# Prompt attention: the value products of two neighbouring units in one run of TensorE and one PSUM bank

## The chip, the cores and the metric

The kernel runs on one core of one Trainium2 chip. The metric is device time in microseconds (us) of one execution. The core has five engines that each work through their own row of instructions in order, and wait for one another through semaphores: TensorE (PE, matmuls, with the weight loads shown apart as PEld), VectorE (DVE), ScalarE (ACT), GpSimd (POOL) and SyncE (SP, which issues DMAs).

## What is computed

The reference is one inference step of a decoder layer with two kinds of heads (forgetting attention and a matrix memory), for one prompt of 2048 tokens and for 64 new tokens of eight older sequences; then an output projection, layer norms and an MLP. The change touches only the forgetting attention of the prompt: 8 heads of 64 columns, 2048 queries and keys, causal, with a decay that is a difference of running sums of log forget values.

```python
def _fox_prompt(q, k, v, logf):
    L = jnp.cumsum(logf, axis=1).transpose(0, 2, 1)
    ...
    def block(args):
        q_i, L_i, i = args
        s = jnp.einsum('bqhd,bkhd->bhqk', q_i, k).astype(jnp.float32) * scale
        s = s + L_i[..., :, None] - L[:, :, None, :]
        q_pos = i * Q_BLOCK + jnp.arange(Q_BLOCK)
        s = jnp.where(k_pos[None, :] <= q_pos[:, None], s, -jnp.inf)
        p = jax.nn.softmax(s, axis=-1)
        return jnp.einsum('bhqk,bkhd->bqhd', p.astype(v.dtype), v)
    ...
...
    mix = jnp.concatenate([fox_h, mn.astype(x.dtype)], axis=-1) @ w_o
```

## The kernel before

The program has stages one after the other: projections and the matrix memory, then the prompt attention (`phase_b`), the output projection, the MLP. Beside them runs, in slices, the attention over the paged cache of the older sequences. A tile framework gives every tile its buffer from a ring of so many buffers (`bufs=`), adds the waits, and sets the order of each engine's row when the program is built, by a simulated timeline; on the chip each engine keeps to its row.

The prompt attention goes over 64 units: 8 heads (h) by 8 groups (g) of 256 queries. A unit (h, g) has the keys 0 to 256(g + 1) - 1, so its work grows with g. The loop over n issues `scores` of unit n, then `values` of unit n - 1 (LA = 1).

`scores`: for each of the unit's two rows of 128 queries and each 512 keys, two matmuls (L1028 and L1029) put the products of the split queries `qh`, `ql` with the rounded keys `ks` into a score bank `pS`; there are three such banks. DVE adds the decay `nl` (L1036; on the diagonal `nd`, with the causal mask, L1040), keeps the largest value of each row in `mx`, and writes the tile `S` in SBUF (7 buffers of 128 x 1024).

`values`: ACT takes the exponential of `S` in place, with the row sums as a by-product (L1057); DVE gathers them (L1058, `ls`). PE turns each 128 x 128 piece of `S` by a transpose (L1073) into `pt`, up to four pieces in a bank, three such banks. ACT (L1076) or DVE (L1078) copies them to `PT` (4 buffers of 128 x 4 x 256). When the unit's last transpose is issued, the value products follow (L1083): 2g + 2 matmuls with 64 columns of values `vn` against 256 queries, even key blocks in rows 0 to 63 of the bank `po`, odd ones in rows 64 to 127. Each of these fp32 matmuls leaves two records in the trace. There is one `po` bank. ACT copies its first half to `ot` (L1091) and DVE adds the second half (L1093). After every fourth unit `finish` scales by the reciprocal row sums, through a small round trip in DRAM (`drl`, `rl`), and stores the result (`dmix`).

Around these stand, in each head, the loads of the next head's keys, `kn`, in four pieces, and of each unit's queries `qn`, on SP's queue, with their splits: ACT rounds (L153, to `ks`, `qh`), DVE forms the remainder (L156, the lower half of `ks`, and `ql`). A key piece can be split once the buffer of keys is free. GpSimd forms `nd` and sums output weights of the MLP in DRAM.

The output projection reads its weights `w_o` through `raw()`, a ring named `wr` of five tiles of 128 x 1024; `half_wo` loads one of them. Before the change five such loads are in the program at n = 60, and SP's row has them among the first loads of the stage.

Places of the names: `raw` is

```python
        return pcw.tile([128, 1024], F32, name="wr", bufs=5)
```

and `tc.issue_after(turned.ins)` keeps a product behind the named transpose in PE's row.

Of the kernel before, what the change touches and what calls it, by code (L numbers as in the profile page):

```python
# [10 lines left out]
F32 = mybir.dt.float32  # L11
# [3 lines left out]
OP = mybir.AluOpType  # L15
# [37 lines left out]
def body(ctx, tc, I, O, stages):  # L53
    nc = tc.nc
    V, A, G, T, SY = nc.vector, nc.scalar, nc.gpsimd, nc.tensor, nc.sync
# [51 lines left out]
    last = {}  # L107
# [821 lines left out]
    for bi in range(4):  # L929
        g = block_a(bi)  # L930
# [20 lines left out]
    def phase_b():  # L951
        es = ExitStack()
        pb = es.enter_context(tc.tile_pool(name="pb", bufs=1, reuse_waits="tile"))
        ppb = es.enter_context(tc.tile_pool(name="ppb", bufs=1, space=PSUM, reuse_waits="tile"))
# [92 lines left out]
        def values(z, g, sc):  # L1047

            if z["h"] == 0 and g == 0:
                pad(pb, 64)  # L1050
            for i, (st, mx) in enumerate(sc):
                qt = 2 * g + i
                n = (qt + 1) * 128
                lp = pb.tile([128, 2], F32, name="lp", bufs=6)
                for k, sp in enumerate(st):
                    w = min(1024, n - k * 1024)
                    last["ACT"] = A.activation(sp[:, :w], sp[:, :w], AF.Exp, bias=mx[:, 7:8], accum_out=lp[:, k:k + 1])  # L1057
                V.tensor_reduce(z["ls"][:, qt:qt + 1], lp[:, :len(st)], axis=AX.X, op=OP.add)  # L1058

            po = ppb.tile([128, 256], F32, name="po", bufs=1)  # L1060
            nk = 2 * g + 2
            PTs = []
            for k0 in range(0, nk, 4):
                PT = pb.tile([128, 4, 256], F32, name="PT", bufs=4)
                PTs.append(PT)
                for i in range(2):
                    kk = min(4, 2 * g + i + 1 - k0)
                    if kk <= 0:
                        continue
                    pt = ppb.tile([128, 4, 128], F32, name="pt", bufs=3)  # L1070
                    for k in range(kk):
                        c = k0 % 8 * 128 + k * 128
                        turned = T.transpose(pt[:, k], sc[i][0][k0 // 8][:, c:c + 128], ident)  # L1073
                    dst = PT[:, :kk, i * 128:i * 128 + 128]
                    if i == 0 or (k0 // 4) % 2 != 0:
                        A.copy(dst, pt[:, :kk])  # L1076
                    else:
                        V.tensor_copy(dst, pt[:, :kk])  # L1078
            for k in range(nk):
                q0 = 128 if k == nk - 1 else 0  # L1080
                c = (k % 2) * 64
                with tc.issue_after(turned.ins):
                    last["PE"] = T.matmul(po[c:c + 64, q0:], z["vn"][:, k], PTs[k // 4][:, k % 4, q0:],  # L1083
                                          start=(k < 2), stop=(k >= nk - 2), skip_group_check=True)
            if g % 4 == 0:
                z["ot"] = pb.tile([64, 1024], F32, name="ot", bufs=2)
            od = z["ot"][:, (g % 4) * 256:(g % 4) * 256 + 256]
            if (z["h"], g) == units[-1]:
                V.tensor_copy(od, po[0:64])
            else:  # L1090
                A.copy(od, po[0:64])  # L1091
            q0 = 128 if g == 0 else 0
            V.tensor_tensor(od[:, q0:], od[:, q0:], po[64:128, q0:], op=OP.add)  # L1093
            if g % 4 == 3:
                finish(z, g // 4)

        def finish(z, half):

            h, ls, ot = z["h"], z["ls"], z["ot"]
            lr = pb.tile([128, 32], F32, name="lr", bufs=2)  # L1100
            V.reciprocal(lr, ls)
            lt = pb.tile([128, 32], F32, name="lt", bufs=2)
            V.transpose(lt, lr)
            o = half * 1024
            for a in range(4):
                SY.dma_start(drl[h, o:o + 1024].rearrange("(t a q) -> a t q", a=4, q=32)[a], lt[a * 32 + half * 8:a * 32 + half * 8 + 8])
            for q in range(2):
                rl = pb.tile([64, 512], F32, name="rl", bufs=2)
                SY.dma_start(rl, dap(drl, h * S + o + q * 512, [[0, 64], [1, 512]]))
                s = slice(q * 512, (q + 1) * 512)  # L1110
                end = (h, half) == (7, 1)
                (V if end else G).tensor_tensor(ot[:, s], ot[:, s], rl, op=OP.mult)
                (G if end else SY).dma_start(dmix[h // 2, (h % 2) * 64:(h % 2) * 64 + 64, o + q * 512:o + q * 512 + 512], ot[:, s])
# [15 lines left out]
        G.affine_select(dmask, dmask, pattern=[[-1, 128]], compare_op=OP.is_ge, fill=NEG, base=0, channel_multiplier=1)  # L1129
        keys(Z[0], 0, bf["kn"])  # L1130
        sc = {}
        w2_due = [0.0]
        LA = 1
        for n in range(len(units) + LA):
            if 10 <= n < 16 and acc[1] is not None:
                attend()
            w2_due[0] += 64 * (n % 8 // 2 + 1) / 130 if n >= 8 else 0
            while n and len(w2_done) < min(60 if False else 64, w2_due[0]):
                w2_sum()
            if n == 60:  # L1140
                wo.extend(half_wo(*q) for q in ((0, 0), (0, 1), (0, 2), (0, 3), (1, 0)))
            if n < len(units):
                h, g = units[n]
                sc[n] = scores(Z[h], g)
                if h == 0 and g % 2 == 0 and g < 6:
                    keys(Z[0], g // 2 + 1)
                if h < 7:
                    if g == 3:
                        Z[h + 1] = head(h + 1)
                        forget_values(Z[h + 1], 0, S)  # L1150
                    if g >= 4:
                        keys(Z[h + 1], g - 4)
                if n + 1 < len(units):
                    queries(Z[units[n + 1][0]], units[n + 1][1])
            if n >= LA:
                h, g = units[n - LA]
                values(Z[h], g, sc.pop(n - LA))
# [15 lines left out]
    def raw():  # L1173

        return pcw.tile([128, 1024], F32, name="wr", bufs=5)
# [9 lines left out]
    def w2_sum():  # L1185

        k = len(w2_done)
        w2_done.append(k)
        j, src, q, more = W2_SUMS[k // 8]
        with tc.issue_after(last["POOL"].ins):  # L1190
            G.dma_start(dw2[k % 8, j], src[k % 8, q], **({"accum_op": OP.add} if more else {}))

    def half_wo(hf, q):

        r = raw().rearrange("p (k c) -> p k c", k=2)
        SY.dma_start(r, I["w_o2"][hf, q].rearrange("p (k c) -> p k c", k=2))
        return r
# [445 lines left out]
def sample_attention(tc, I, O, ps_, pps, cst, ident, dnl, dR, dmix, dqb, vx, kx, pa):  # L1643
# [218 lines left out]
    def weights(b, u, hg):  # L1862

        z = state[b]
        if hg == 0:
            z["PT"] = ps_.tile([128, 2, 4, 4, 4, 8], F32, name="PTs", tag="PTs", bufs=1)
        PT = z["PT"]
        p = pps.tile([128, 4, 128], F32, name="sT", tag="sX", bufs=1)
        for f in range(4):
            T.transpose(p[:, f], z["U"][u][:, hg, f].rearrange("p k t -> p (k t)"), ident)  # L1870
        for f in range(4):
            (A.copy if f % 2 else V.tensor_copy)(PT[:, hg, f].rearrange("p g h q -> p h g q"),
                                                 p[:, f].rearrange("p (h g q) -> p h g q", g=4, q=8))
# [22 lines left out]
    def pv_step(b, kt, after):  # L1896
# [164 lines left out]
```

## Time and profile before

| what | value |
|---|---|
| runs, median of 3 | 3192.88 us (3190.92 to 3194.03) |
| profiled execution, span from first to last instruction | 3196.6 us (the record gives no other time for it) |
| mean granted clock of TensorE | 0.989 |
| DVE, ACT busy over the span | 65%, 45% |
| prompt attention in the trace | 869 to 1308 us |
| in that stretch, busy: PE, DVE, ACT | 418.0, 345.7, 330.5 of 439.0 us |
| its transposes (PE, L1073) | 1088 |
| its value products (PE, L1083), records | 1152 |

A row of the timeline gives the start, the duration, the engine, the line, the operation with output and inputs, and how many instructions it joins; in brackets stands the idle time before it and what ended that. The durations of matmuls overlap, so that the distance between two starts is the better price of one. A row of the windows gives the window, its length, and the busy time of PE, PEld, DVE, ACT and POOL with the number of instructions, then the granted clock (1.00 is full speed), the share of the DMA engines, and GB/s. A row of the waits gives the waiting instruction, the one that it waited for, the us in total, how often, and the longest.

### The profile page before, as it was taken

To read this page: it belongs to the slowest core of one execution; us is meant where nothing else is said; L and a number is where in the kernel's file an instruction comes from. 1 tells how busy PE (TensorE), PEld (TensorE's weight loads), DVE (VectorE), ACT (ScalarE), POOL (GpSimd) and SP (SyncE) were. 2 spreads that over 40 slices of the span, in tenths; PEclk is the share of its full clock that TensorE was granted. 3 is DMA by queue.
4 is the path that set the end of the run, shared out by engine and by line. 5 is a ranking of instruction groups with operands and counts; after the bars stand their busy time and mean duration, and the time that the engine had idled before them with its cause. 6 is when DMAs were issued, how large, how long until landed. Compare 5 with 4: busy or idle time off the path is not lost.

```text
span 3196.6 us, 53750 instructions
## 1 busy us (share of the span) xinstructions
PE 3103.8 (97%) x19869; PEld 2442.8 (76%) x19869; DVE 2081.3 (65%) x5025; ACT 1439.5 (45%) x2629; POOL 907.0 (28%) x976
## 2 busy tenths in 40 slices
PE   8999999999999999999999999999999999899998
PEld 8997787787667667777777777777766777698886
DVE  6956467465488778534657568565675665766667
ACT  3343244344387777422444445343444444344442
POOL 0121132423433333466333324333334111000000
PEclk9999999999999999999999999999999999999999
DMA  5565666877787865687877879878779766643231
GB/s 191 155 213 181 236 225 202 277 261 237 245 260 178 204 152 139 223 297 259 314 291 271 308 243 335 312 270 323 290 262 332 276 213 208 209 155 132 101 123 63
DMA packets 323615, 732.58 MB, mean 229 GB/s; under 512 B 63097, under 2 KB 153721, under 8 KB 322457
## 3 DMA queue, kind: packets, MB, share of 16 engines
q1 hardware_dynamic: 235928, 413.36, 39.3%
q0 software_dynamic: 83808, 304.91, 27.6%
q10 hardware_dynamic: 3616, 10.88, 0.9%
q8 instruction: 157, 2.57, 0.3%
q14 instruction: 106, 0.86, 0.1%
HBM read 676.20 MB, written 86.38 MB: 239 GB/s over the span
## 4 chain that ended last, share of the span: by engine, by line
PE 47%; DMA 4%; DVE 1%; issue 1%; POOL 1%; ACT 0%; DVEq 0%; POOLq 0%; ACTq 0%
PE ph L162 7%; PE ph L164 7%; PE ph L163 7%; PE py L162 6%; PE py L163 6%; PE py L164 6%; PE sO L1913 3%; DMA vt<-cache_v,idxV 2%; PE sQ L1801 2%; PE ph L169 1%; PE sT L1870 1%; DMA kT<-cache_k,idxK 1%; DMA xr<-cache_v,idxV 0%; DVE wl L156 0%; PE pw L163 0%
## 5 line engine op out<-in xcount | busy, mean ns | idle before, releaser
L156 DVE TENSOR_TENSOR wl<-wr,wh 128x1024 fp32r<-128x1024 f32 x300 | 366.3, 1223 | 241.3 <-ACT wh L153 240.3
L153 ACT ACTIVATE wh<-wr 128x1024 fp32r<-128x1024 f32 x300 | 315.8, 1055 | 336.7 <-PE py L164 160.7
L162 PE MATMUL ph<-x1h,wh 128*128 128x512 f32 (+1 forms) x1280 | 455.5, 356 | 0.0
L163 PE MATMUL ph<-x1l,wh 128*128 128x512 f32 (+1 forms) x1280 | 453.6, 355 | 0.2 <-DVE x1l L156 0.2
L164 PE MATMUL ph<-x1h,wl 128*128 128x512 f32 (+1 forms) x1280 | 451.7, 355 | 0.5 <-DVE wl L156 0.3
L1778 POOL DMA_INDIRECT kT<-cache_k,idxK x256 | 277.4, 1084 | 555.7 <-PE sQ L1801 490.3
L162 PE MATMUL py<-wh,hh 128*128 128x512 f32 x900 | 357.5, 402 | 7.1 <-DVE y L1427 4.5
L163 PE MATMUL py<-wl,hh 128*128 128x512 f32 x900 | 353.7, 394 | 0.0
L164 PE MATMUL py<-wh,hl 128*128 128x512 f32 x900 | 350.3, 393 | 0.4 <-DVE hl L156 0.4
L1427 DVE TENSOR_TENSOR y<-y,py 128x512 f32<-128x512 f32 x410 | 277.8, 683 | 97.0 <-PE py L164 92.9
L1889 POOL DMA_INDIRECT vt<-cache_v,idxV x164 | 179.0, 1091 | 398.9 <-PE sO L1913 337.5
L162 PEld LDWEIGHTS ph<-x1h,wh 128*128 128x128 f32 x1280 | 241.5, 189 | 39.7 <-issue 7.0
L164 PEld LDWEIGHTS ph<-x1h,wl 128*128 128x128 f32 x1280 | 240.8, 189 | 36.5 <-issue 3.7
L163 PEld LDWEIGHTS ph<-x1l,wh 128*128 128x128 f32 x1280 | 241.7, 189 | 35.3 <-issue 4.1
L162 PE MATMUL pm<-xh,whi 128*128 128x512 f32 (+2 forms) x640 | 232.2, 363 | 0.0
L164 PE MATMUL pm<-xh,wlo 128*128 128x512 f32 (+2 forms) x640 | 229.7, 359 | 0.0
L163 PE MATMUL pm<-xl,whi 128*128 128x512 f32 (+2 forms) x640 | 228.4, 357 | 0.0
L162 PEld LDWEIGHTS py<-wh,hh 128*128 128x128 f32 x900 | 168.8, 189 | 60.1 <-issue 21.8
L162 PE MATMUL pm<-whi,xh 128*128 128x256 f32 (+4 forms) x624 | 202.3, 325 | 7.9 <-ACT whi L153 7.9
L156 DVE TENSOR_TENSOR wlo<-wra,whi 128x1024 fp32r<-128x1024 f32 (+1 forms) x112 | 140.8, 1258 | 102.7 <-ACT whi L153 102.3
L163 PE MATMUL pm<-wlo,xh 128*128 128x256 f32 (+4 forms) x624 | 200.4, 321 | 0.6 <-DVE wlo L156 0.6
L164 PE MATMUL pm<-whi,xl 128*128 128x256 f32 (+4 forms) x624 | 199.9, 321 | 0.6 <-DVE xl L156 0.6
(378 smaller groups left out, 6461.2 us busy)
## 6 DMA issues: line engine op xcount, KB each, us to landing
wr<-w SPq DMA_DIRECT2D x200, 512.0 KB
wra<-w_in SPq DMA_DIRECT2D x104, 512.0 KB
wr<-dw SPq DMA_DIRECT2D x96, 512.0 KB
dw<-w POOLq DMA_DIRECT2D x48, 512.0 KB, 7.2
Rb<-dR SPq DMA_DIRECT2D x128, 128.0 KB
kT<-dw SPq DMA_DIRECT2D x28, 512.0 KB
kT<-w SPq DMA_DIRECT2D x25, 512.0 KB
xn<-xp_t SPq DMA_DIRECT2D x16, 512.0 KB
```

The costliest lines, as they stand in the source:

```text
L153: last["ACT"] = A.activation(dst, src, AF.Copy, scale=scale)
L156: r = (eng or V).tensor_tensor(dst, src, hi.bitcast(F32), op=OP.subtract)
L162: T.matmul(ps, wh, xh, start=first, stop=False, skip_group_check=shared)
L163: T.matmul(ps, wh, xl, start=False, stop=False, skip_group_check=shared)
L164: last["PE"] = T.matmul(ps, wl, xh, start=False, stop=stop, skip_group_check=shared)
L169: last["PE"] = T.matmul(ps[n * 64:n * 64 + 64], w, x, start=first, stop=stop, skip_group_check=True)
L1427: V.tensor_tensor(y, y, ps, op=op)
L1778: G.indirect_dma_start(out=piece(n), out_offset=None, in_=ck, in_offset=IO(ap=idxK[:, b, j // 2, j % 2:j % 2 + 1], axis=0))
L1801: r = T.matmul(pq[h4 * 32:h4 * 32 + 32, hg].rearrange("p (k c) -> p k c", k=2), z["qb"][:, hd], kv, start=(db == 0), stop=(db == 1), skip_ ...
L1870: T.transpose(p[:, f], z["U"][u][:, hg, f].rearrange("p k t -> p (k t)"), ident)
L1889: vx["last"] = G.indirect_dma_start(out=vt.rearrange("p f c -> p (f c)"), out_offset=None, in_=cv, in_offset=IO(ap=idxV[:, b, (kt % 4) * 4 ...
L1913: after_ = T.matmul(po[r:r + 32], z["PT"][:, hg, 2 * f + g, pg].rearrange("p h q -> p (h q)"), vts[f][:, g, hg * 256:(hg + 1) * 256], star ...
```

## The change

Units are taken in pairs, g even with the next odd g, except in the last half of the last head. The even unit does its exponentials, transposes and copies, puts its turned tiles on the list `held`, and returns. The odd unit's turned tiles go into tiles of the `wr` ring in place of `PT`. After the odd unit's last transpose the products of both units are issued, into one `po` bank of 512 columns, 256 for each unit. One ACT copy of 64 x 512 and one DVE add take the place of two of 256. Since the ring `wr` is in use until the last pair, the five early loads of `w_o` move behind it (n = 61 in place of 60).

```diff
-            po = ppb.tile([128, 256], F32, name="po", bufs=1)
             nk = 2 * g + 2
+            pair = z["h"] < 7 or g < 4
             PTs = []
             for k0 in range(0, nk, 4):
-                PT = pb.tile([128, 4, 256], F32, name="PT", bufs=4)
+                if pair and g % 2:
+                    PT = raw().rearrange("p (k c) -> p k c", k=4)
+                else:
+                    PT = pb.tile([128, 4, 256], F32, name="PT", bufs=4)
                 PTs.append(PT)
...
-            for k in range(nk):
-                q0 = 128 if k == nk - 1 else 0
-                c = (k % 2) * 64
-                with tc.issue_after(turned.ins):
-                    last["PE"] = T.matmul(po[c:c + 64, q0:], z["vn"][:, k], PTs[k // 4][:, k % 4, q0:],
-                                          start=(k < 2), stop=(k >= nk - 2), skip_group_check=True)
-            if g % 4 == 0:
+            held.append((g, nk, PTs))
+            if pair and g % 2 == 0:
+                return
+            po = ppb.tile([128, 512], F32, name="po", bufs=1)
+            a = len(held) * 256
+            for i, (u, nk, PTs) in enumerate(held):
+                for k in range(nk):
+                    q0 = 128 if k == nk - 1 else 0
+                    c = (k % 2) * 64
+                    with tc.issue_after(turned.ins):
+                        last["PE"] = T.matmul(po[c:c + 64, i * 256 + q0:i * 256 + 256], z["vn"][:, k], PTs[k // 4][:, k % 4, q0:],
+                                              start=(k < 2), stop=(k >= nk - 2), skip_group_check=True)
+            u = held[0][0]
+            held.clear()
+            if u % 4 == 0:
                 z["ot"] = pb.tile([64, 1024], F32, name="ot", bufs=2)
-            od = z["ot"][:, (g % 4) * 256:(g % 4) * 256 + 256]
+            od = z["ot"][:, u % 4 * 256:u % 4 * 256 + a]
...
-                A.copy(od, po[0:64])
-            q0 = 128 if g == 0 else 0
-            V.tensor_tensor(od[:, q0:], od[:, q0:], po[64:128, q0:], op=OP.add)
+                A.copy(od, po[0:64, :a])
+            q0 = 128 if u == 0 else 0
+            V.tensor_tensor(od[:, q0:], od[:, q0:], po[64:128, q0:a], op=OP.add)
...
-            if n == 60:
+            if n == 61:
                 wo.extend(half_wo(*q) for q in ((0, 0), (0, 1), (0, 2), (0, 3), (1, 0)))
```

With the change the lines shift: transposes stand in L1076, their copies in L1079 (ACT) and L1081 (DVE), the products in L1092, the evacuation in L1102, the add in L1104, the loads of `w_o` in L1208.

PE's row where one head gives way to the next (`vn` with a number is a head's values, `ks` its keys) is this before, with the products of the ending head's last unit:

```order
L1073 MATMUL pt<-ident,S 128x128 x7
L1083 MATMUL po<-PT,vn_10275 64x256 x8
L1028 MATMUL pS<-ks_11056,qh 128x384
L1029 MATMUL pS<-ks_11056,ql 128x384
L1028 MATMUL pS<-ks_11056,qh 128x512
L1029 MATMUL pS<-ks_11056,ql 128x512
L1083 MATMUL po<-PT,vn_10275 64x256 x4
L1073 MATMUL pt<-ident,S 128x128 x4
L1028 MATMUL pS<-ks_11056,qh 128x512
L1029 MATMUL pS<-ks_11056,ql 128x512
L1083 MATMUL po<-PT,vn_10275 64x256
L1083 MATMUL po<-PT,vn_10275 64x128
```

At the same place of the changed kernel PE's row is:

```order
L1076 MATMUL pt<-ident,S 128x128 x4
L1028 MATMUL pS<-ks_11029,qh 128x512
L1029 MATMUL pS<-ks_11029,ql 128x512
L1076 MATMUL pt<-ident,S 128x128 x11
L1092 MATMUL po<-PT,vn_10260 64x256 x13
L1092 MATMUL po<-PT,vn_10260 64x128
L1092 MATMUL po<-wr,vn_10260 64x256 x15
L1092 MATMUL po<-wr,vn_10260 64x128
L1076 MATMUL pt<-ident,S 128x128 x6
```

The products of units 6 and 7 of a head, 30 matmuls, now stand in one piece behind the last transposes of unit 7; before they were in pieces between score pairs and transposes of the next head.

ACT's row at that place before (`ks` with a number is a later head's keys):

```order
L1091 COPY ot<-po 64x256
L1076 COPY PT<-pt 128x4x128 x3
L153 ACTIVATE qh<-qn 128x256
L153 ACTIVATE ks_12606<-kn 128x512 x3
L153 ACTIVATE qh<-qn 128x256
L1076 COPY PT<-pt 128x128
L1076 COPY PT<-pt 128x2x128
L1057 ACTIVATE S,lp<-S,mx 128x1024 x2
L1057 ACTIVATE S,lp<-S,mx 128x128
L1057 ACTIVATE S,lp<-S,mx 128x256
L153 ACTIVATE qh<-qn 128x256
L1076 COPY PT<-pt 128x4x128
```

And ACT's row there with the change:

```order
L153 ACTIVATE ks_11792<-kn 128x512 x3
L1079 COPY PT<-pt 128x4x128
L1079 COPY PT<-pt 128x128
L153 ACTIVATE qh<-qn 128x256
L1057 ACTIVATE S,lp<-S,mx 128x1024 x2
L1079 COPY PT<-pt 128x2x128
L153 ACTIVATE qh<-qn 128x256
L1057 ACTIVATE S,lp<-S,mx 128x128
L1057 ACTIVATE S,lp<-S,mx 128x256
L1057 ACTIVATE S,lp<-S,mx 128x384
L1079 COPY wr<-pt 128x4x128 x3
L153 ACTIVATE ks_11792<-kn 128x512
```

The work is the same; the copies of the odd unit's tiles stand in one group further back, between the small exponentials of the next head and the fourth key split.

SP's row near the end of the stage, with the change; the loads of `w_o` stood before among the first `kn` and `qn` loads of the stage:

```order
L1117 DMA drl<-lt 8x32 x4
L1208 DMA wr<-w_o 128x1024 x2
L1120 DMA rl<-drl 64x512 x2
L1208 DMA wr<-w_o 128x1024 x3
L1124 DMA dmix<-ot 64x512 x2
```

They are now issued between the small transfers of `finish` for a half of the last head.

More of the change, by code (lines that the diff above doesn't have):

```diff
@@ L1078, in values @@
                         V.tensor_copy(dst, pt[:, :kk])
-            for k in range(nk):
-                q0 = 128 if k == nk - 1 else 0
-                c = (k % 2) * 64
-                with tc.issue_after(turned.ins):
-                    last["PE"] = T.matmul(po[c:c + 64, q0:], z["vn"][:, k], PTs[k // 4][:, k % 4, q0:],
-                                          start=(k < 2), stop=(k >= nk - 2), skip_group_check=True)
-            if g % 4 == 0:
+            held.append((g, nk, PTs))
[13 more added lines that the diff above has]
+            if u % 4 == 0:
                 z["ot"] = pb.tile([64, 1024], F32, name="ot", bufs=2)
-            od = z["ot"][:, (g % 4) * 256:(g % 4) * 256 + 256]
+            od = z["ot"][:, u % 4 * 256:u % 4 * 256 + a]
             if (z["h"], g) == units[-1]:
-                V.tensor_copy(od, po[0:64])
+                V.tensor_copy(od, po[0:64, :a])
             else:
-                A.copy(od, po[0:64])
-            q0 = 128 if g == 0 else 0
-            V.tensor_tensor(od[:, q0:], od[:, q0:], po[64:128, q0:], op=OP.add)
+                A.copy(od, po[0:64, :a])
+            q0 = 128 if u == 0 else 0
+            V.tensor_tensor(od[:, q0:], od[:, q0:], po[64:128, q0:a], op=OP.add)
             if g % 4 == 3:
@@ L1131, in phase_b @@
         sc = {}
+        held = []
         w2_due = [0.0]
```

## The prediction

> **What bounds the kernel now.** I read the page's busy times first, then the mean of each engine by stretches of one head, then what TensorE (PE) waits for in the prompt attention, then the timeline of PE, VectorE (DVE) and ScalarE (ACT) where one head gives way to the next.
>
> ```profile
> span 3196.6 us, 53750 instructions
> PE 3103.8 (97%) x19869; PEld 2442.8 (76%) x19869; DVE 2081.3 (65%) x5025; ACT 1439.5 (45%) x2629; POOL 907.0 (28%) x976
> 973.60:1024.80 51.20, 50.95 (x361) 36.61 (x360) 43.77 (x172) 40.37 (x96) 19.17 (x31) 1.00 0.79 196
> 1076.80:1135.20 58.40, 53.24 (x361) 37.22 (x360) 43.90 (x175) 42.30 (x101) 18.64 (x33) 0.97 0.65 180
> 1135.20:1193.60 58.40, 52.99 (x361) 37.61 (x360) 43.03 (x174) 40.93 (x97) 19.50 (x31) 0.94 0.74 177
> PE pt L1073 <- ACT PT L1076: 9.7, 4, 5.2
> ```
>
> PE is busy 97% of the span. In a head of the prompt attention (third row: window, length, then busy time of PE, weight loads, DVE, ACT, GpSimd, the granted clock, DMA) PE works 50.95 of 51.20 us, DVE 43.77, ACT 40.37. So PE bounds the stage, but DVE has only 15% to spare over a head: work that is badly spread can turn this round. Here is PE, and below DVE and ACT, around one change of head:
>
> ```profile
> 1028.93 0.39 PE L1029 MATMUL pS<-ks,ql 128*128 128x512 f32 x1
> 1029.26 1.08 PE L1083 MATMUL po<-PT,vn 128*64 128x256 f32 x8
> 1030.27 0.66 PE L1073 MATMUL pt<-ident,S 128*128 128x128 f32 x4
> 1030.68 0.48 PE L1028 MATMUL pS<-ks,qh 128*128 128x512 f32 x1
> ...
> 1034.69 0.39 PE L1029 MATMUL pS<-ks,ql 128*128 128x512 f32 x1
> 1034.93 0.60 PE L1073 MATMUL pt<-ident,S 128*128 128x128 f32 x4
> 1035.28 0.36 PE L1028 MATMUL pS<-ks,qh 128*128 128x256 f32 x1
> 1035.48 0.28 PE L1029 MATMUL pS<-ks,ql 128*128 128x256 f32 x1
> 1035.60 0.40 PE L1028 MATMUL pS<-ks,qh 128*128 128x512 f32 x1
> 1035.83 0.40 PE L1029 MATMUL pS<-ks,ql 128*128 128x512 f32 x1
> 1036.44 1.14 PE L1073 MATMUL pt<-ident,S 128*128 128x128 f32 x7 [0.21 <-ACT PT L1076]
> 1037.52 2.81 PE L1083 MATMUL po<-PT,vn 128*64 128x256 f32 x24
> 1040.26 0.33 PE L1073 MATMUL pt<-ident,S 128*128 128x128 f32 x1
> ```
> ```profile
> 1029.27 1.29 DVE L156 TENSOR_TENSOR ks<-kn,ks 64x512 fp32r<-64x512 f32 x2
> 1030.60 0.43 DVE L156 TENSOR_TENSOR ql<-qn,qh 128x256 fp32r<-128x256 f32 x1
> 1030.94 0.42 DVE L1036 CUSTOM_DVE_ANT_0 S<-pS,nl 128x256 f32<-128x256 f32 x1
> 1031.28 0.08 DVE L1036 DVE_READ_ACCUMULATOR2_ANT mx<- 128x1 f32 x1
> ...
> 1032.60 0.69 DVE L1078 COPY PT<-pt 128x512 f32<-128x512 f32 x1
> 1033.20 0.41 DVE L156 TENSOR_TENSOR ql<-qn,qh 128x256 fp32r<-128x256 f32 x1
> 1033.53 0.55 DVE L1036 CUSTOM_DVE_ANT_0 S<-pS,nl 128x384 f32<-128x384 f32 x1
> ...
> 1034.01 0.29 DVE L1040 CUSTOM_DVE_ANT_0 S<-pS,nd 128x128 f32<-128x128 f32 x1
> 1034.22 0.15 DVE L1058 TENSOR_REDUCE ls<-lp 128x1 f32<-128x1 f32 x1
> 1034.29 0.68 DVE L1036 CUSTOM_DVE_ANT_0 S<-pS,nl 128x512 f32<-128x512 f32 x1
> 1034.89 0.08 DVE L1036 DVE_READ_ACCUMULATOR2_ANT mx<- 128x1 f32 x1
> ...
> 1035.22 0.42 DVE L1093 TENSOR_TENSOR ot<-ot,po 64x256 f32<-64x256 f32 x1
> 1035.56 0.14 DVE L1043 TENSOR_REDUCE mx<-mx 128x1 f32<-128x2 f32 x1
> ```
>
> Starts, not durations, give the price of one in a row. **PE:** a value matmul takes (1040.26 - 1037.52 - 1.01) / 16 = 0.108 us a record, the 1.01 being the run of 8 from 1029.26 to 1030.27. Entering a run costs 0.09 (0.33 after a score matmul at 1028.93, against 0.24 into a transpose at 1034.69), the run itself 1.01 - 8 x 0.108 = 0.15 more than its records, the step out 0.06 (0.41 for four transposes at 1030.27, 0.35 at 1034.93): **0.30 us for each run**. A score pair of 512 is 2 x 0.23, of 256 2 x 0.12, of 384 about 0.36 (between them), a transpose 0.108 (as the value record). **DVE:** score tile of 512 0.60, 384 0.48, 256 0.34, 128 0.21; copy of a turned tile 0.60; half key split 0.66; query split 0.33; final add 0.34 for 256 columns, so some 0.6 for 512.
>
> **The change, part by part.** *Fewer runs.* The order of instructions has 95 runs of value products before and 63 after, with the same 576 value products (1152 records), 1088 transposes and 320 score pairs. 32 x 0.30 = **-9.5 us**. The rows of a head priced in this way (28 pairs of 512, 4 of 384, 8 of 256, 136 transposes, 144 records, 12 runs) give 12.9 + 1.4 + 1.9 + 14.7 + 15.6 + 3.6 = 50.1 us, against 51.20: 1.1 us of a head are small waits such as the 0.21 above.
>
> The Trainium skill, "TensorEngine Tiling (Array Packing)", Key Properties, says that a change of tiling mode drains the array. The 0.33 against 0.24 at 1028.93 and 1034.69 agrees; by that rule alone the change gives its -9.5 and nothing else, which is rival A. "Perfetto Trace Analysis", Optimizing Tensor Performance, Matmuls, speaks the other way: independent matmul groups should rotate through PSUM banks so that the evacuation of one overlaps the next group's matmuls. Putting two units in one bank and run works against it.
>
> *What the runs covered.* While PE runs value products, DVE and ACT have time for scores, exponentials, copies and key splits. In the order before, the runs are scattered among the score pairs and transposes (8, 4, 24 above). After, all products of units 4 and 5 stand in one run of 22 matmuls, those of 6 and 7 in one of 30, and between them PE has 9 score pairs of 512, 2 of 384, 4 of 256 and 58 transposes: 9 x 0.46 + 2 x 0.36 + 4 x 0.24 + 58 x 0.108 = **12.1 us**. In the same stretch DVE's order has the add of the pair just ended, 5 tiles of 512, 2 of 384, 2 of 256, 8 of 128, 4 copies of 512, 4 half key splits, 3 query splits, and some 15 small reductions at 0.06 to 0.27: 0.6 + 3.0 + 1.0 + 0.7 + 1.7 + 2.4 + 2.6 + 1.0 + 1.4 = **14.4 us**, all of it ahead of the copy whose bank the last transposes need. It can't begin before the first new score pair (0.6), and four transposes follow it (0.4): the run of 30 begins 15.5 after the end of the run of 22. **PE waits 3.4 us.** The product run can't start earlier, since each product is held behind the odd unit's last transpose.
>
> ```profile
> 1026.17 1.67 ACT L153 ACTIVATE ks<-kn 128x512 fp32r<-128x512 f32 x3
> 1028.44 1.16 ACT L1057 ACTIVATE S<-S,mx 128x1024 f32<-128x1024 f32 x1
> 1035.29 0.63 ACT L153 ACTIVATE ks<-kn 128x512 fp32r<-128x512 f32 x1 [1.46 <-DMA kn<-k_prompt]
> 1035.83 1.05 ACT L1076 COPY PT<-pt 128x512 f32<-128x512 f32 x2
> ```
>
> ACT has in that stretch, from the first turned tile to the fourth key split, 4 exponentials of 1024 or 896 (4.5), 3 small ones (1.5, an estimate from the same row by columns), 7 copies of 512 (3.4), two small (0.4), 3 query splits (0.9) and 4 key splits (2.1): 12.8 us. It starts some 2.0 after the run's end (first score pairs and transposes), and then DVE's split (0.66), the copy (0.60) and four transposes (0.43) follow: 16.5, so PE waits **4.4**. Walking the three rows step by step, with every bank and its reader, gave me 17.4, a wait of **5.3**. I take 4.4, the middle one, for 6 changes of head: **+26.4** (bounds 20.4 to 31.8). The change of head without key splits (into the last one) gets **+1.0** (0 to 2): 2.6 us less on DVE, 2.1 on ACT. During the 6.6 us of the run of 30 both engines have little to do, so nothing of this wait is paid back there.
>
> *Before the run of 22* PE has 11 pairs of 512, 2 of 256 and 38 transposes: 5.1 + 0.5 + 4.1 = 9.7 us; DVE has ten tiles of 512, one of 384, four of 128, three copies, a query split and small ones: 6.0 + 0.5 + 0.8 + 1.5 + 0.3 + 0.5 = 9.6, starting late by the evacuation ahead of it. I count 0.5 us in 7 heads, **+3.5** (0 to 7).
>
> *Waits that were there already.* The 1.1 us of a head lie mostly at this same change of head; the new wait takes them in. Half of them, over 7 heads: **-4** (-8 to 0).
>
> ```profile
> 891.10 1.06 SPq L1196 DMA_DIRECT2D wr<-w_o  x2
> 893.39 1.53 SPq L1196 DMA_DIRECT2D wr<-w_o  x3
> ```
>
> *The five loads of output weights* leave the start of the stage, where key, value and query loads run on the same queue: **-1.5** (-3 to 0; ACT's whole wait for key loads is bounded by rows such as the 1.46 above). They are issued behind the last paired products, half a head (some 25 us by the rows above) before their first reader; 2.6 MB at the 177 GB/s in the last column of the windows take 15 us, so nothing there. *Evacuations:* one of 512 columns takes the place of two of 256; both engines save a little, which DVE's sum above has in it. *A new wait* is that of products on the pair's single bank: behind it on PE stand transposes, but 10 to 12 us lie between two pairs and the evacuation with its add takes about 1.1: nothing.
>
> **Sum:** -9.5 + 26.4 + 1.0 + 3.5 - 4 - 1.5 = **+15.9 us** on the profiled execution's span of 3196.6. That span stands 3.7 above the median of the runs, 3192.9, so I add the sum to the median: about **3208.5**. With all bounds at their lower ends: -9.5 + 20.4 + 0 + 0 - 8 - 3 = 0 (3193); at their upper ends +31.3 (3224).
>
> **Rivals.** *A, the waits stay hidden.* If DVE and ACT work further ahead than I count (the ring of turned tiles has five more buffers now), PE stays the bound and the 9.5 come in full: **3183**. For it: 50.95 of 51.20, and DVE's 43.77. It decides from the point where 3.4 us of DVE's list of 14.4 (five or six score tiles) are done before the run of 22 ends. Against it: three score banks and three banks of turned tiles allow no more lead than before. *B, the key loads.* Two heads have 58.4 us, and PE's waits for ACT's copies (9.7 in total) hold most of it: ACT stands at a key split whose load is late. If the moved loads or the longer rows end that, up to 14 us go: **3195**; if it strikes one head more, +6.5: **3215**. Neither has a row that decides it. *C, slower by the clock:* if the new wait comes in one piece.
>
> ```profile
> 1093.22 1.33 PE L1073 MATMUL pt<-ident,S 128*128 128x128 f32 x7 [4.00 <-ACT PT L1076]
> 1094.48 4.26 PE L1083 MATMUL po<-PT,vn 128*64 128x256 f32 x24
> ```
>
> After 4.00 us of waiting, seven transposes and 24 records took 5.59 us, where the same rows at 1036.44 took 3.95: 1.64 more, in 6 heads +9.8: **3218**. It decides from a single wait somewhere between the 0.25-us kind and 4.00; I expect mine in two or three pieces, since the three score banks stop PE before the last transposes do. The Trainium skill, "TensorE: Matmul & The Clock Gate", has the clock halved after an idle window of about 3.4 us; the row agrees, and by it a single wait of 4.4 would pay rival C's price. *D, loads late:* the output weights come after their reader, up to +5: **3213**.
>
> **How the numbers follow.** Forecast 0.50 (3193 to 3224), A 0.16, B 0.06 for each side, C 0.17, D 0.05. A measurement of this kernel can tell about 0.2%, 6.4 us, from no change. Faster by that: A and a little of the forecast's and B's lower ends, 0.18. Same: the lower third of the forecast and half of B, 0.19. Slower: the rest, 0.63. The range runs from A's time to C with the upper bounds' half: 3183 to 3228.
>
> **What would show it.** Right: each change of head has PE idle before transposes for 3 to 5 us in sum, released by DVE's or ACT's copies; a head lasts 53 to 55 us; DVE and ACT idle while the run of 60 records lasts 6.6 us. The first term is right if 63 runs are there and a record still takes 0.108. Wrong: heads of 48 to 49 us with PE waiting under 1 us (A), a granted clock under 1.00 in the run of 60 (C), ACT waiting for output weights at the start of the output projection (D), and waits for key loads other than before's (B). The forecast falls if DVE's work of that stretch turns out to be spread into the run of 22 ahead of it.

## The result, and the profile after

| | before | after |
|---|---|---|
| median of 4 runs | 3193.45 us (3190.92 to 3195.08) | 3243.28 us (3235.87 to 3248.97) |
| ratio, with its 95% interval | | 1.0157 (1.0143 to 1.0170) |
| profiled execution, span | 3196.6 us | 3241.2 us |
| of it the prompt attention (first score matmul to first matmul of the output projection) | 439.0 us | 478.1 us |

The change makes the kernel 1.6% slower, some 50 us. The prediction had the sign and a third of the size: 3208.5, with 3228 as its upper end. The page of the changed kernel begins:

```profile
span 3241.2 us, 53691 instructions
PE 3117.7 (96%) x19869; PEld 2459.1 (76%) x19869; DVE 2080.6 (64%) x4995; ACT 1439.1 (44%) x2599; POOL 909.7 (28%) x976
```

The same matmuls keep PE busy 14 us longer, although there are 32 fewer runs to enter and leave; DVE and ACT have the same work as before. The eight heads of the prompt attention, in the windows view of the changed kernel (window, length, busy PE, PEld, DVE, ACT, GpSimd, then granted clock, DMA share, GB/s):

```profile
862.30:916.10 53.80, 45.82 (x265) 31.68 (x266) 41.71 (x160) 35.31 (x79) 13.84 (x25) 0.90 0.56 166
916.10:973.60 57.50, 52.94 (x365) 38.92 (x363) 44.35 (x169) 40.75 (x94) 25.39 (x37) 0.97 0.72 230
973.60:1032.00 58.40, 52.95 (x362) 38.67 (x361) 43.67 (x169) 40.93 (x93) 19.45 (x31) 0.97 0.67 172
1032.00:1090.80 58.80, 53.07 (x363) 38.79 (x362) 42.07 (x169) 40.87 (x94) 20.74 (x31) 0.97 0.78 171
1090.80:1150.60 59.80, 54.48 (x364) 40.01 (x362) 42.84 (x169) 40.92 (x95) 18.39 (x31) 0.94 0.58 160
1150.60:1213.70 63.10, 54.23 (x362) 38.66 (x361) 42.21 (x169) 40.89 (x93) 19.88 (x31) 0.95 0.67 159
1213.70:1276.20 62.50, 57.10 (x364) 42.56 (x362) 44.49 (x169) 41.34 (x95) 19.35 (x31) 0.89 0.59 148
1276.20:1340.40 64.20, 63.14 (x455) 44.58 (x453) 43.70 (x177) 49.16 (x108) 14.46 (x23) 1.00 0.46 121
```

The first and the last head are little changed: they took 52.6 us (clock 0.90) and 63.2 (1.00) before. Of the six between them, four took 51 to 52 us before, at a clock of 1.00, and two took 58.4. Now all six are at 57 to 63, and in every one of the six the clock is under 1.00. Loss of clock and waiting have come together. PE at one change of head, in the timeline of the changed kernel (in the last row the run of units 6 and 7 begins, 60 records with those that follow):

```profile
1035.52 0.66 PE L1076 MATMUL pt<-ident,S 128*128 128x128 f32 x4
1037.13 0.66 PE L1076 MATMUL pt<-ident,S 128*128 128x128 f32 x4 [0.95 <-ACT S L1057]
1038.79 1.86 PE L1076 MATMUL pt<-ident,S 128*128 128x128 f32 x8 [1.01 <-DVE ls L1058]
1040.67 0.80 PE L1028 MATMUL pS<-ks,qh 128*128 128x512 f32 x1
1041.26 0.63 PE L1029 MATMUL pS<-ks,ql 128*128 128x512 f32 x1
...
1043.15 0.93 PE L1076 MATMUL pt<-ident,S 128*128 128x128 f32 x7
1046.82 0.66 PE L1076 MATMUL pt<-ident,S 128*128 128x128 f32 x4 [2.74 <-DVE wr L1081]
1047.41 3.24 PE L1092 MATMUL po<-PT,vn 128*64 128x256 f32 x28
```

Three things are to be seen. PE waits 0.95 and 1.01 for the exponentials of the last units and for DVE, as forecast. Eight transposes then take 1.86 where 1.04 is usual, and the second matmul of the next score pair 0.63 where 0.40 is: the clock is halved. And the last four transposes wait 2.74 for a copy by DVE. Why DVE is late there, ACT's and DVE's rows show:

```profile
1044.69 0.63 ACT L153 ACTIVATE ks<-kn 128x512 fp32r<-128x512 f32 x1 [3.00 <-DMA kn<-k_prompt]
1045.35 0.69 DVE L156 TENSOR_TENSOR ks<-kn,ks 64x512 fp32r<-64x512 f32 x1 [3.50 <-ACT ks L153]
1046.07 0.69 DVE L1081 COPY wr<-pt 128x512 f32<-128x512 f32 x1
```

The fourth key piece of a head comes late; ACT stands at its split, DVE behind ACT, and the copy that PE waits for behind that split.

To divide the 39.1 us by which the stage grew, I priced each row of PE by the distance from its start to the next start. What the same neighbours take in the median at full clock is work; what is over is a wait, or, inside a stretch of half clock, up to twice the price, loss of clock. A wait comes out a little longer this way than in brackets, which count idle time only from a matmul's modelled end. In us, for the stage (I call this the ledger):

| kernel | stage | work | waits | clock |
|---|---|---|---|---|
| before | 439 | 405 | 27 | 7 |
| after | 478 | 398 | 61 | 19 |

So -7 by fewer runs, **+34 by waits, +11 by half clock**, and 1 of rounding. This is an estimate from one traced execution of each kernel: with the prices drawn somewhat differently the three come out at -4, +32 and +11.

### The profile page after: what moved, and what is told of

It reads as the page before. It is cut to its first block, busy times and chain, and to the rows that moved or that the text cites. A ratio compares the mean times of both kernels' runs of the same rounds, so it can differ in the third digit from the quotient of the medians.

```text
span 3241.2 us, 53691 instructions
## 1 busy us (share of the span) xinstructions
PE 3117.7 (96%) x19869; PEld 2459.1 (76%) x19869; DVE 2080.6 (64%) x4995; ACT 1439.1 (44%) x2599; POOL 909.7 (28%) x976
```

## The experiments

Each time is beside runs of the kernel before on the same chip, whose medians were 3195.9, 3193.0 and 3200.4 in the three groups; the ratios are to those.

**1. The side effects alone.** The kernel before, with the ring for the odd units' turned tiles and the late loads of output weights:

```diff
-                PT = pb.tile([128, 4, 256], F32, name="PT", bufs=4)
+                if (z["h"] < 7 or g < 4) and g % 2:
+                    PT = raw().rearrange("p (k c) -> p k c", k=4)
+                else:
+                    PT = pb.tile([128, 4, 256], F32, name="PT", bufs=4)
...
-            if n == 60:
+            if n == 61:
```

> The kernel before, with the two side effects of the change alone: the odd units' turned tiles lie in the ring of output weights, and the five early loads of w_o come late. Every unit's products are issued behind its own transposes, in a bank of 256 columns; 94 runs. Theory (the gathered value products cost the time, since they no longer cover DVE and ACT): about the kernel before, 3193 (3186 to 3199), no PE wait over 2 us except for late key loads. Rival (the ring or the late loads cost it): 3220 or more, with ACT waiting for w_o or PE waiting for a tile of the ring.

Measured: 3204.15 (10 runs), ratio 1.0021 (1.0007 to 1.0036), just outside what I expected of the theory and far from the rival's. The stage takes 442 us, 3 more than before. So the ring and the late loads are not the cause of the 50 us; together they cost some 7.

**2. One bank, each unit at its own pace.** The shared bank and the shared evacuation stay, but the even unit's products are issued behind its own transposes:

```diff
-            held.append((g, nk, PTs))
-            if pair and g % 2 == 0:
-                return
-            po = ppb.tile([128, 512], F32, name="po", bufs=1)
...
+            po = held[0][1] if held else ppb.tile([128, 512], F32, name="po", bufs=1)
+            i = len(held)
+            held.append((g, po))
+            for k in range(nk):
...
+            if pair and g % 2 == 0:
+                return
```

> The change, with one bank and one evacuation for two units, but the even unit's products issued behind its own transposes in place of the odd unit's: 113 runs. Theory: 18 runs more than before at 0.30 us, +5, so 3199 (3192 to 3206); no wait at the change of head beyond those of before. Rival (the shared bank, whose next products wait for the evacuation, is what costs): near 3240, with PE waiting in front of the products.

Measured: 3213.45, ratio 1.0056 (1.0034 to 1.0078); above the theory's range, but not the rival's 3240. The stage takes 445 us: work 409, so 18 runs more cost 4 (0.2 a run), waits 30, clock 5. PE's waits in front of products for the evacuation are 0.8 us in all:

```profile
PE po L1089 <- DVE ot L1104: 0.8, 2, 0.4
```

So the bank is not the cause: it is the gathering of the products that makes the difference between this kernel's 18 us and the 50. Of the 18, the ring and the late loads with 7 and the runs with 4 leave some 7 without a cause. The traced execution, of 3203.75 us, can't show them: it is the shortest of the four, the others took 3212 to 3216.

**3 to 5. Which pairs.** The pairs without that of units 6 and 7; only units 6 and 7; only units 4 and 5:

```diff
-            pair = z["h"] < 7 or g < 4
+            pair = g < 6 and z["h"] < 7 or g < 4
```
```diff
-            pair = z["h"] < 7 or g < 4
+            pair = z["h"] < 7 and g >= 6
```
```diff
-            pair = z["h"] < 7 or g < 4
+            pair = z["h"] < 7 and 4 <= g < 6
```

> The change without the pair of units 6 and 7, whose run of 30 stands behind the change of head: 91 runs. Theory: the waits at the change of head (2.7 to 8.6 us in each of six heads of the changed kernel, 29 in sum) and the halved clock behind them go, and the waits ahead of the run of 22 mostly too, since that run is broken up as well: 3190 to 3207. Rival (the single waits ahead of the run of 22, or late key loads, make up the loss): over 3220.

> Only units 6 and 7 paired: 64 runs. Theory: the waits at the change of head stay (some 29 us, with the halved clock 6 to 12), the runs give -9.5, the single waits ahead of the run of 22 go: 3215 to 3232. Rival (the change of head costs little, the run of 22 and what stands ahead of it the rest): 3190 to 3205.

> Only units 4 and 5 paired: 83 runs, one of 22 in each head, with the products of units 6 and 7 at their own pace behind it. Theory (it is the stretch without any product from the run of 22 to that of 30 which costs, and either pair alone leaves products in it): a small loss like that of the kernel with units 6 and 7 alone or less, 3195 to 3210; ahead of the run of 22 PE waits about 0.9 us a head, more where a query split meets GpSimd's multiplication. Rival (the run of 22 by itself carries the part of the loss that units 6 and 7 alone do not, some 35 us of the 50): 3215 to 3235.

| kernel | median, ratio | stage | work | waits | clock |
|---|---|---|---|---|---|
| without units 6, 7 | 3205.42, 1.0028 (1.0015 to 1.0042) | 442 | 405 | 33 | 3 |
| units 6, 7 only | 3210.74, 1.0044 (1.0032 to 1.0056) | 449 | 396 | 45 | 10 |
| units 4, 5 only | 3205.29, 1.0018 (1.0006 to 1.0030) | 442 | 401 | 31 | 10 |

The pair of units 6 and 7 alone costs 15 us of time, less than the 22 to 39 that I expected from the changed kernel's waits at the change of head (3215 to 3232 was written); the other two kernels fell within their ranges. In the kernel with units 6 and 7 alone the waits at a change of head are these, in its timeline:

```profile
1033.55 0.92 PE L1076 MATMUL pt<-ident,S 128*128 128x128 f32 x6 [0.60 <-DVE mx L1043]
1035.74 0.66 PE L1076 MATMUL pt<-ident,S 128*128 128x128 f32 x4 [0.80 <-ACT S L1057]
1037.05 0.36 PE L1028 MATMUL pS<-ks,qh 128*128 128x256 f32 x1 [0.66 <-DVE mx L1040]
1038.50 1.97 PE L1076 MATMUL pt<-ident,S 128*128 128x128 f32 x8 [0.34 <-DVE mx L1043]
```

2.4 us in four pieces, each behind DVE or ACT, and behind them again half clock: 1.97 for eight transposes. That is the mechanism of the prediction. But neither pair, nor both losses together (15 and 5), nor this pair's with that of the kernel without it (15 and 9, which take in every pair), reach 50: with all pairs something joins. Two candidates stood in the changed kernel's trace, the late key loads above, and this, in DVE's and GpSimd's rows ahead of a run of 22:

```profile
1013.42 2.46 DVE L156 TENSOR_TENSOR ql<-qn,qh 128x256 fp32r<-128x256 f32 x1
```
```profile
1013.72 1.87 POOL L1123 TENSOR_TENSOR ot<-ot,rl 64x512 f32<-64x512 f32 x1
1014.94 1.23 POOL L1021 TENSOR_TENSOR nd<-nl,dmask 128x128 f32<-128x128 f32 x1
```
```profile
1016.61 0.50 PE L1028 MATMUL pS<-ks,qh 128*128 128x512 f32 x1 [2.80 <-DVE mx L1036]
```

A query split, 0.41 us elsewhere, takes 2.46 beside GpSimd's work, and PE waits 2.80.

**6. Four buffers for key pieces, in both kernels.** So that the fourth load of a head need not wait for the first piece's split (two small tiles of `finish` have one buffer in place of two):

```diff
-            kn = kns.pop() if kns else pb.tile([128, 512], F32, name="kn", bufs=3)
+            kn = kns.pop() if kns else pb.tile([128, 512], F32, name="kn", bufs=4)
...
-            lr = pb.tile([128, 32], F32, name="lr", bufs=2)
+            lr = pb.tile([128, 32], F32, name="lr", bufs=1)
...
-            lt = pb.tile([128, 32], F32, name="lt", bufs=2)
+            lt = pb.tile([128, 32], F32, name="lt", bufs=1)
...
-        kns = [pb.tile([128, 512], F32, name="kn", bufs=3)]
+        kns = [pb.tile([128, 512], F32, name="kn", bufs=4)]
```

> The changed kernel with four buffers for key pieces in place of three (two small tiles of finish have one buffer in place of two), so that the fourth key piece of a head need not wait for the first one's split. Theory (of the waits at the change of head, those for the fourth key split, 0.5 to 5.3 us in five heads and 11 in sum, are late loads): they go, with some of the half clock: 3224 to 3238. Rival (DVE's and ACT's own work ends last there whatever the loads do): 3240 to 3250.

> The kernel before with four buffers for key pieces. Its waits for late key loads are 4.2 and 5.3 us in two heads, which last 58.4 in place of 51 to 52 us with the halved clock behind them. Theory: both heads come down to 52: 3178 to 3188. Rival (the loads are late for another reason, the queue or its neighbours): 3190 to 3199.

Measured on the changed kernel: 3222.58, ratio 1.0091 (1.0074 to 1.0108), 21 us of the 50 gone, a little more than expected. ACT's waits for key pieces fall from 15.3 us to 3.0, in the waits view of the changed kernel and of this one:

```profile
ACT ks L153 <- DMA kn<-k_prompt: 15.3, 8, 4.4
```
```profile
ACT ks L153 <- DMA kn<-k_prompt: 3.0, 3, 1.7
```

On the kernel before: 3194.37 (10 runs), ratio 1.0005 (0.9990 to 1.0020): no gain that can be measured, although its profiled run, of 3186.66 us, has the stage at 432 in place of 439, and the two heads at 52 and 53 in place of 58.4. The forecast for it was wrong. Only this run was traced, and its mean clock of 0.993 is that of the three shortest of the ten (3186 to 3189); the other seven had 0.987 to 0.992 and took 3193 to 3206. So the clock, which differs from run to run of one kernel, goes with most of the spread; whether the shorter stage is there in the seven isn't known.

**7. Without GpSimd's multiplication.** The outputs of all but the last half head are not multiplied by the reciprocal row sums:

```diff
-                (V if end else G).tensor_tensor(ot[:, s], ot[:, s], rl, op=OP.mult)
+                V.tensor_tensor(ot[:, s], ot[:, s], rl, op=OP.mult) if end else None
```

> The changed kernel without GpSimd's multiplication of the heads' outputs by the reciprocal row sums (left out in all but the last half head). In the changed kernel DVE's query split takes 1.8, 2.5 and 2.7 us in three places, where it else takes 0.41, each time beside such a multiplication, and PE then waits 2.3, 3.0 and 3.2 us ahead of the run of 22 (with smaller ones 12 us in sum). Theory (the two engines get in each other's way, and the gathered runs no longer hide it): no query split over 1.1 us, these waits gone, half clock less: 3222 to 3236. Rival (DVE's row itself is late there): 3240 to 3250, the waits stay.

Measured: 3235.98, ratio 1.0139 (1.0122 to 1.0156), 7 us less than the changed kernel. In its profile a query split at the same place takes its usual time:

```profile
1018.24 0.41 DVE L156 TENSOR_TENSOR ql<-qn,qh 128x256 fp32r<-128x256 f32 x1
```

The waits ahead of the run of 22, between 0.96 and 3.22 us in the changed kernel's six heads and 12.5 in sum, are now 0.90 to 0.93 in each, 5.5 in sum (by distances of starts): the 0.9 are DVE's own row, the other 7 were GpSimd's doing. Of the stage's 63 query splits, eight took 0.85 to 2.71 us in the changed kernel; here one takes 0.99 and the rest at most 0.43. The stage gained only 4 us; this run had more late key loads (ACT waits 20.7 us for them in place of 15.3), which would account for the rest.

**8. Both.** Four buffers for key pieces, and no multiplication on GpSimd (the edits of 6 and 7):

> The changed kernel with both: four buffers for key pieces, and without GpSimd's multiplication of the outputs by the reciprocal row sums. Theory: late key loads (21 us with their clock) and the blocked query splits (7 us) add up, and what is left is the stretch's own work on DVE and ACT, some 4 us at each change of head and 0.9 ahead of each run of 22, less 9 for the runs saved: 3207 to 3217. Rival (the two hide each other, one taking the place of the other): 3219 to 3225, as with the four buffers alone.

Measured: 3228.43 (four runs, 3216.92 to 3229.34), ratio 1.0076 (1.0046 to 1.0105): by the median slower than with the four buffers alone, by the ratio 5 us faster, with intervals that overlap. It was predicted at 3207 to 3217 if the two gains add up and at 3219 to 3225 if one hides the other, so it lies above both. The kernel before ran 7 us slower here than in the group before, which would bring the two forecasts to 3214 to 3224 and 3226 to 3232, and 3228.43 into the second. So by times alone the two gains can't be told to add up. The stage tells more: 462 us, against 467 with the buffers and 474 without the multiplication. One head of it, in the windows view and PE's waits in it:

```profile
1029.30:1086.60 57.30, 54.05 (x362) 39.76 (x361) 42.15 (x169) 40.97 (x94) 15.59 (x27) 0.94 0.79 175
```
```profile
1033.37 0.66 PE L1076 MATMUL pt<-ident,S 128*128 128x128 f32 x4 [0.48 <-ACT PT L1079]
1034.98 0.92 PE L1076 MATMUL pt<-ident,S 128*128 128x128 f32 x4 [0.95 <-ACT S L1057]
1036.73 1.97 PE L1076 MATMUL pt<-ident,S 128*128 128x128 f32 x8 [0.83 <-DVE ls L1058]
```

The three waits are all that is left at this change of head, none over 1 us, and still the clock is 0.94.

**9. Work put into the gap.** The products of unit 6 are issued once more, behind unit 6's own transposes; the later run writes over them:

```diff
             held.append((g, nk, PTs))
+            if pair and g == 6:
+                po = ppb.tile([128, 512], F32, name="po", bufs=1)
+                for k in range(nk):
+                    q0 = 128 if k == nk - 1 else 0
+                    c = (k % 2) * 64
+                    with tc.issue_after(turned.ins):
+                        T.matmul(po[c:c + 64, q0:256], z["vn"][:, k], PTs[k // 4][:, k % 4, q0:],
+                                 start=(k < 2), stop=(k >= nk - 2), skip_group_check=True)
+                z["po"] = po
...
-            po = ppb.tile([128, 512], F32, name="po", bufs=1)
+            po = z.pop("po", None) or ppb.tile([128, 512], F32, name="po", bufs=1)
```

> The changed kernel, with the 14 products of unit 6 issued once more, behind unit 6's own transposes, into the same bank (the later run writes over them): 21 runs and 98 matmuls more, at 0.216 us each and 0.30 a run some 27 us of PE's work, all of it at the change of head. Theory (PE has nothing to do there and waits for DVE and ACT, and the clock is halved because of the idle pieces): the waits shrink by about what is added, and the half clock in the stage (47.8 us in the changed kernel, 19 us lost) with them, so 3230 to 3250, the same as the changed kernel or faster. Rival (PE's own rows bound that stretch): the 27 us come on top, 3265 or more.

Measured: 3241.65, ratio 1.0154 (1.0122 to 1.0186): 98 more matmuls in 21 more runs, and no more time that could be measured. The head that stood above at 58.80 us and a clock of 0.97 is now, in the windows view of this kernel:

```profile
1038.00:1095.90 57.90, 54.36 (x390) 39.41 (x389) 42.38 (x169) 40.77 (x94) 20.74 (x31) 1.00 0.78 174
```

27 more matmul records, full clock, 0.9 us less. So PE's added work found a place at the change of head that was idle or half-clocked before. The stage by the ledger, all kernels of 6 to 9 (in us):

| kernel | stage | work | waits | clock |
|---|---|---|---|---|
| before, four key buffers | 432 | 405 | 23 | 4 |
| after, four key buffers | 467 | 398 | 53 | 16 |
| after, no multiplication | 474 | 398 | 62 | 13 |
| after, both | 462 | 398 | 48 | 16 |
| after, products of unit 6 twice | 477 | 426 | 45 | 6 |

In the last row the 28 us of added work took 16 from the waits and 12 from the loss of clock. That holds for the traced run, of 3235.97 us with a mean clock of 0.991. Of the other three, one was like it (3230.54, 0.991), and two took 3247 and 3249 at 0.987 and 0.986, so not every run keeps its clock. Whether the half clock alone would give its 12 us back, with nothing added, these runs don't separate.

## Why the prediction was wrong, and where it was right

The sum came to +15.9 (on a median of 3192.9 that is 3208.8, not 3208.5), and the measured change is +50. By the ledger the 34 us between them are: some 2.5 for runs that cost less than 0.30 each, 9 for waits, 11 for half clock, which the sum put at nothing, 1 of rounding, and 11 that lie outside the prompt attention.

*Fewer runs, -9.5:* right in kind, a little too large. The order's 32 runs gave -7 by the ledger, and the 18 more runs of experiment 2 cost +4: some 0.2 us for each run.

*The new wait at the change of head, +26.4, with +1.0 and +3.5 beside it and -4 for the waits that were there:* 26.9 in sum. As DVE's and ACT's own work it was right. With key loads and multiplication out of the way (both edits, waits of 48) against the kernel before with early key loads (23), the waits grew by 25; and in the kernel with both edits the second to sixth changes of head wait 3.5 to 4.5 us each by the ledger, where 4.4 was forecast. The place was right too: PE stands before transposes, for DVE and ACT, in pieces of 0.4 to 1.1 us.

*The step that failed first* is the -4: "the new wait takes them in". The late key loads did not vanish in the new wait; they came on top of it. Before, ACT waited 15.9 us for key pieces, and PE lost about 9.5 to it, in two heads; after, ACT waited 15.3, and PE lost 11 in five heads. The same holds for the query splits blocked beside GpSimd: the kernel before had one of 2.00 us at 1016.06 that cost PE nothing, since eight transposes, a score pair and a value run lay ready for it:

```profile
1016.06 2.00 DVE L156 TENSOR_TENSOR ql<-qn,qh 128x256 fp32r<-128x256 f32 x1
```

In the changed kernel two of 2.5 and 2.7 cost PE 3.0 and 3.2. In sum the waits grew by 34 and not by 25; I take the other 9 for disturbances that the kernel before hides or feels less. That is argued from the two traces: the kernel before was not run without the multiplication. I had priced the stretch with DVE's usual durations only, and a stretch with no spare work pays for every late guest.

*The second failed step, and the larger one,* is rival C's condition. I had put half clock behind "a single wait somewhere between the 0.25-us kind and 4.00", and expected mine in pieces, so the sum has nothing for it. The pieces came as expected and the clock was halved all the same, once at each of the six changes of head with key splits (at one of them a single wait of 5.10 us stands there too), for 3.4 us at three and 6.8 at the other three, and once ahead of a run of 22: 11 us more, near rival C's 9.8. So its price came close, and the point from which it decides was wrong. In its place the traces show a share of busy time: where PE is busy for less than about half of a stretch of 3.4 us, half clock follows, as the last section works out.

*The loads of output weights, -1.5:* no gain is to be seen. The first head took 53.8 in place of 52.6, and the kernel with the ring and the late loads alone was 7 us slower. *D, loads late:* did not happen. ACT waits for output weights in the output projection, but it did before: 10.1 us before, 10.9 after, 8.9 and 9.4 of them in one wait. The output projection took 230.4 in place of 226.5 us in the profiled run, but 226.1 with the ring and the late loads alone.

*Rival A* is refuted: six heads of 57 to 63, not 48 to 49. *Rival B's* dearer half happened, in other heads.

*What is left:* the stage explains 39 of the 44.6 us between the two profiled runs and of the 50 between the medians. In the profiled runs the stage before it was 6.7 us shorter and those behind it 12.2 longer, though PE, DVE and ACT carry out the same instructions in the MLP, a few of them in another order. The MLP took 1662.1 us before and 1670.4 after. Of these 8 us, 7 are longer waits of PE for the tiles of the paged cache that come by DMA (18.3 us for `vt` in place of 13.5, 3.6 for `xr` in place of 2.8, 3.2 for `kT` in place of 2.0). The MLP took 1660 to 1662 us in the two kernels with early loads of output weights, and 1665 to 1677 in the ten others that were profiled. That is a hint, not a cause: why these tiles come later in the changed kernel's traced run, and whether by the late loads or by chance, is open.

## What to carry to other kernels

Before gathering small runs of an engine, ask which engine they cover and add up that engine's row in the stretch that loses its cover: 14.4 us of DVE against 12.1 of PE was enough to turn a gain of 7 us into a loss. Then add what the cover also hid, late loads and contention among them; the buffers that make loads early should come first, since they took back 21 of the 50 us here, and made no difference where the cover still stood. And an engine that wins nothing from being fast in a stretch can be given work there for nothing: 98 matmuls cost no time here.

## What the runs showed of the hardware

The granted clock fell to half without any long wait. In the windows view of the changed kernel, in steps of 2 us around the change of head above:

```profile
1034.00:1036.00 2.00, 1.85 (x9) 1.09 (x8) 1.97 (x8) 2.00 (x6) 2.00 (x4) 1.00 0.93 377
1036.00:1038.00 2.00, 0.83 (x6) 0.42 (x4) 1.91 (x5) 2.00 (x3) 0.38 (x1) 1.00 1.02 240
1038.00:1040.00 2.00, 1.21 (x6) 1.21 (x7) 1.71 (x7) 2.00 (x9) 0.12 (x1) 0.74 1.02 182
1040.00:1042.00 2.00, 1.98 (x8) 1.31 (x7) 1.84 (x13) 1.69 (x5) 0.77 (x2) 0.50 1.02 223
1042.00:1044.00 2.00, 2.00 (x15) 1.70 (x14) 0.00 (x0) 0.00 (x0) 1.74 (x3) 0.91 1.03 288
```

PE was busy 0.83 and then 1.21 of 2 us, with no single wait above 1.01, and the clock went to 0.50 for about 3.4 us (0.26, 0.50 and 0.09 of the three windows lost, 1.7 us in all). The Trainium skill, "TensorE: Matmul & The Clock Gate", What's actually happening, gives an idle window of about 3.4 us as the condition; here a stretch of that length which was half idle did the same.

Where the limit lies can be read from the twelve traces. In each of them the granted clock changes only at times that are whole multiples of 3.41 us apart, so a trace can be cut into stretches of 3.41 us, which lie differently in each. The stretch ahead of the half clock above is this one, with PE busy 1.45 of 3.41 us, or 42%:

```profile
1035.55:1038.96 3.41, 1.45 (x11) 0.97 (x10) 3.28 (x8) 3.41 (x9) 0.83 (x2) 1.00 1.01 239
```

At full clock, all 129 stretches with PE busy for less than 43% were followed by half clock, 34 of the 92 between 43% and 58%, and 4 of the 10,778 above. From half clock, none of the 49 stretches under 75% was followed by full clock, 18 of the 40 between 75% and 95%, and 137 of the 139 above. So a few waits of 1 us that fall into one stretch are enough. These are counts of traces whose matmul ends are modelled; no run varied the idle share on purpose.

DVE's splits, which have two inputs in SBUF, were held up beside GpSimd's element-wise work: 2.46 us in place of 0.41, and back at 0.41 once GpSimd's multiplication was left out. The Trainium skill, "GPSIMD Engine Reference", Specifications, has GpSimd's SBUF interfaces shared with VectorE, with contention for DVE instructions with two SBUF inputs; the run agrees.
